# Row maxima of a 16384 x 1024 matrix: coarser loads, seven rows by way of TensorE and GpSimd, a split last row and a later first store

## The chip, the cores and the metric

The kernel runs on one core of one Trainium2 chip. The metric is the device time of one execution in microseconds; a smaller one is better. Times "from the start" are counted from the beginning of the profiled span.

## The reference

```python
def setup_inputs():
    batch, seq, dim = 32, 512, 1024
    return {
        "x": np.random.randn(batch, seq, dim).astype(np.float32),
    }

def reference(x: np.ndarray) -> np.ndarray:
    return np.max(x, axis=-1).astype(np.float32)
```

The input is 32 x 512 x 1024 float32, 67.1 MB; the output is the maximum of each of the 16384 rows of 1024 elements.

## The kernel before, in words

The 16384 rows are spread over 128 partitions, 128 rows to each. They are cut in two blocks (`BLOCKS`, L13). In the first, partition p holds 112 consecutive rows of the input, in the second 16. Within a block the rows of a partition are brought in by loads of n consecutive rows each: one DMA (L49) brings n x 1024 elements to each of the 128 partitions, n x 4 KB in one piece. The list has 15 loads of 14 down to 3 rows, and then 11 of 2 and 1 rows.

The loads go into `ring` (L37), one tile with room for 46 rows in each partition. `at` is the next free row; where a load doesn't fit before the end, it begins at row 0 again (L46, L47). A load that lands on rows used earlier must wait until the reductions of those rows are done. The scheduler puts that wait on SP, which issues all loads in the order of the list; it also gives each DMA one of eight completion semaphores in turn, and a DMA that gets a semaphore again waits for the one that had it before.

For each load VectorE runs one `reduce_max` over the free dimension (L50): n maxima per partition from n x 1024 elements, written into `res` (L38), 128 columns of one value each. VectorE works on the loads in their order and waits for each load's semaphore. No other engine computes. ScalarE issues the two stores (L54), each behind its block's last reduction: 112 values of each partition, and 16.

So three queues set the order: SP's list of loads, VectorE's list of reductions, and ScalarE's two stores. TensorE and GpSimd have nothing but the start and the end of the program.

Of the kernel before, what the change touches and what calls it, by code (L numbers as in the profile page):

```python
# [1 line left out]

# [4 lines left out]


F32 = mybir.dt.float32

BLOCKS = [  # L13
    [14, 14, 12, 11, 9, 8, 8, 7, 6, 5, 4, 4, 4, 3, 3],
    [2, 2, 2, 2, 2, 1, 1, 1, 1, 1, 1],
]
RING = 46


@with_exitstack  # L20
def kernel(
    ctx: ExitStack,
    tc: tile.TileContext,
    x: bass.AP,
    out: bass.AP,
):
    nc = tc.nc
    P = 128
    X = mybir.AxisListType.X

    xf = x.flatten_outer_dims()
    N, D = xf.shape
    I = N // P
    of = out.flatten_outer_dims()

    once = ctx.enter_context(tc.tile_pool(name="once", bufs=1))
    ring = once.tile([P, RING, D], F32)  # L37
    res = once.tile([P, I], F32)  # L38

    at = first = 0  # L40
    for loads in BLOCKS:
        S = sum(loads)
        xb = xf[first * P:(first + S) * P, :].rearrange("(p i) d -> p i d", p=P)
        b = 0
        for g in loads:
            if at + g > RING:  # L46
                at = 0  # L47
            xc = ring[:, at:at + g, :]
            nc.sync.dma_start(out=xc, in_=xb[:, b:b + g, :])  # L49
            nc.vector.reduce_max(out=res[:, first + b:first + b + g], in_=xc, axis=X)  # L50
            at += g
            b += g
        dst = bass.AP(tensor=of.tensor, offset=of.offset + first * P, ap=[[S, P], [1, S]])
        nc.scalar.dma_start(out=dst, in_=res[:, first:first + S])  # L54
        first += S
    assert first == I


# [1 line left out]
_INS = ['x']  # L60
_OUTS = [((32, 512), 'float32')]


# [23 lines left out]
```

## Time and profile before

| | |
|---|---|
| median of 9 runs | 165.04 us (165.00 to 165.17) |
| the profiled execution, its own time | 165.17 us |
| its span in the profile | 163.4 us |
| VectorE busy | 138.5 us, 26 reductions |
| DMA, loads' queue | 67.11 MB, 96.4% of 16 engines' span |
| first reduction begins | 20.24 us |
| last reduction ends | 160.96 us |
| last store issued | 161.00 us |

How to read it: the profiled span lies within the execution; 1.77 us of its time are outside. A busy share of DMA is the mean over the core's 16 DMA engines. The profile calls VectorE DVE, TensorE PE, ScalarE ACT and GpSimd POOL; "SPq" and "ACTq" are the instruction queues that issue DMAs, which aren't counted as busy. In the groups of instructions `res<-ring` means that `res` is written and `ring` read, and the idle time behind the last bar is what the engine waited just before the group's instructions.

### The profile page before, as it was taken

How to read it: one execution, taken by the hardware profiler on the slowest of the kernel's cores; microseconds unless marked ns; L12 is line 12 of the kernel's file. 1: busy time of each engine (PE TensorE's matmuls, PEld its weight loads, DVE VectorE, ACT ScalarE, POOL GpSimd, SP SyncE). 2: the span in 40 equal slices, each digit the busy share in tenths (PEclk: the TensorE clock that was granted, in tenths of full speed). 3: DMA queues.
4: the chain of work that ended last, by engine and by line, in shares of the span. 5: the costliest groups of instructions: out<-in, count | busy, mean ns of one | idle time of the engine just before them, and what ended most of it. 6: DMA issues, size and time to landing. Idle time of an engine off the chain costs nothing.

```text
span 163.4 us, 109 instructions
## 1 busy us (share of the span) xinstructions
DVE 138.5 (85%) x26; POOL 0.2 (0%) x4
## 2 busy tenths in 40 slices
DVE  0000099968999999999999999999999999999994
POOL 0000000000000000000000000000000000000000
DMA  6999999998899897999989999999999999999980
GB/s 225 449 449 449 449 449 449 449 417 385 385 421 509 353 529 321 433 433 473 441 385 481 417 442 428 413 400 451 416 429 421 437 418 420 421 420 415 407 348 2
DMA packets 4032, 67.18 MB, mean 411 GB/s; under 512 B 704, under 2 KB 704, under 8 KB 1472
## 3 DMA queue, kind: packets, MB, share of 16 engines
q1 hardware_dynamic: 3744, 67.11, 96.4%
q10 hardware_dynamic: 288, 0.07, 0.2%
HBM read 67.11 MB, written 0.07 MB: 411 GB/s over the span
## 4 chain that ended last, share of the span: by engine, by line
DMA 57%; DVE 40%; DVEq 1%; SPq 0%; issue 0%
DMA ring<-in_x_dram 57%; DVE res L50 40%; DVEq L82 1%; SPq L49 0%
## 5 line engine op out<-in xcount | busy, mean ns | idle before, releaser
L50 DVE TENSOR_REDUCE res<-ring 128x1 f32<-128x1024 f32 (+11 forms) x26 | 138.5, 5398 | 22.5 <-DMA ring<-in_x_dram 22.5
L71 POOL MEMSET const-bfloat16-1.0<- 128x1 bf16 x1 | 0.1, 102 | 0.0
L71 POOL MEMSET const-uint8-127<- 128x1 uint8 x1 | 0.1, 101 | 0.0
L71 POOL MEMSET const-float32-0.0<- 128x1 f32 x1 | 0.1, 99 | 0.2 <-issue 0.2
L71 POOL MEMSET const-float32-1.0<- 128x1 f32 x1 | 0.1, 98 | 0.0
## 6 DMA issues: line engine op xcount, KB each, us to landing
ring<-in_x_dram SPq DMA_DIRECT2D x2, 7168.0 KB, 27.7
ring<-in_x_dram SPq DMA_DIRECT2D x2, 4096.0 KB, 31.6
ring<-in_x_dram SPq DMA_DIRECT2D x1, 6144.0 KB, 50.1
ring<-in_x_dram SPq DMA_DIRECT2D x3, 2048.0 KB, 36.8
ring<-in_x_dram SPq DMA_DIRECT2D x1, 5632.0 KB, 29.7
ring<-in_x_dram SPq DMA_DIRECT2D x5, 1024.0 KB, 24.6
ring<-in_x_dram SPq DMA_DIRECT2D x1, 4608.0 KB, 23.6
ring<-in_x_dram SPq DMA_DIRECT2D x1, 3584.0 KB, 38.3
```

Source lines behind the costliest of these rows:

```text
L50: nc.vector.reduce_max(out=res[:, first + b:first + b + g], in_=xc, axis=X)
L71: nc = _bacc.Bacc("TRN2", target_bir_lowering=False, num_devices=1)
L82: with _tile.TileContext(nc) as tc:
```

## The change

The lists of loads change: 22 whole loads (15, 15, 15, 15, 14, 11, 11, 8, 4, 4 rows, then three of 2 and nine of 1) instead of 26, and the very last row of each partition comes in two loads of half a row. The ring has 45 rows instead of 46.

The last row: the first half goes to the ring and its maximum is written to the element just ahead of the second half in a tile `tail`; the last reduction then covers that element and the second half, 513 elements.

Seven rows of each partition no longer go through VectorE's long reductions: the last two rows of load seven (11 rows), the last three of load eight (8 rows) and the last two of load ten (4 rows). For each such row `turn` has TensorE transpose eight 128 x 128 pieces into PSUM, ScalarE copy the 128 x 1024 result to SBUF, and GpSimd take the maximum over the partitions with an all-reduce. After it element c x 128 + p of every partition is the maximum of piece c of partition p's row. `back` has TensorE turn the eight 1 x 128 pieces of partition 0 into columns of a small PSUM tile, and a short VectorE reduction over eight values per row (the merge) writes the maxima into `res`. The merges stand on VectorE's queue after loads nine, thirteen and seventeen. TensorE's and VectorE's orders are fixed by hand (`in_turn`). An identity matrix for the transposes is made on VectorE ahead of the first reduction, in eight instructions. The program of GpSimd gains a library reload ahead of seven all-reduces, that of ScalarE a table load and seven copies.

The first block's store is issued behind the reduction of the last whole row, and the second block's store follows it, both still on ScalarE's queue.

```diff
 BLOCKS = [
-    [14, 14, 12, 11, 9, 8, 8, 7, 6, 5, 4, 4, 4, 3, 3],
-    [2, 2, 2, 2, 2, 1, 1, 1, 1, 1, 1],
+    [15, 15, 15, 15, 14, 11, 11, 8, 4, 4],
+    [2, 2, 2, 1, 1, 1, 1, 1, 1, 1, 1, 1],
 ]
-RING = 46
+RING = 45
+TENSOR = {
+    6: [("turn", 6, 0), ("turn", 6, 1), ("back", 6, 0), ("back", 6, 1)],
+    7: [("turn", 7, 0), ("turn", 7, 1), ("turn", 7, 2), ("back", 7, 0), ("back", 7, 1)],
+    9: [("turn", 9, 0), ("turn", 9, 1), ("back", 7, 2), ("back", 9, 0), ("back", 9, 1)],
+}
+BY_GPSIMD = {6: 2, 7: 3, 9: 2}
+MERGE = {8: 6, 12: 7, 16: 9}
...
+    def turn(j, k):
+        rows, cols = tiles[j]
+        ps = psum.tile([P, D], F32)
+        for c in range(C):
+            in_turn("PE", nc.tensor.transpose(
+                out=ps[:, c * P:(c + 1) * P],
+                in_=rows[:, k, c * P:(c + 1) * P],
+                identity=ident,
+            ))
+        sb = turned.tile([P, D], F32)
+        nc.scalar.copy(out=sb, in_=ps)
+        top = allr.tile([P, D], F32)
+        nc.gpsimd.partition_all_reduce(top, sb, P, bass_isa.ReduceOp.max)
+        tops[j, k] = top
+
+    def back(j, k):
+        if j not in backs:
+            fetched = psmall.tile([P, BY_GPSIMD[j], C], F32)
+            backs[j] = fetched
+        for c in range(C):
+            in_turn("PE", nc.tensor.transpose(
+                out=backs[j][:, k, c:c + 1],
+                in_=tops[j, k][0:1, c * P:(c + 1) * P],
+                identity=ident[0:1, 0:1],
+            ))
...
-            nc.vector.reduce_max(out=res[:, first + b:first + b + g], in_=xc, axis=X)
+            cols = res[:, first + b:first + b + n]
+            m = BY_GPSIMD.get(j, 0)
+            tiles[j] = xc[:, n - m:, :], cols[:, n - m:]
+            for what, i, k in TENSOR.get(j, []):
+                (turn if what == "turn" else back)(i, k)
+            reduce = in_turn("DVE", nc.vector.reduce_max(
+                out=cols[:, :n - m], in_=xc[:, :n - m, :], axis=X))
+            if j in MERGE:
+                i = MERGE[j]
+                in_turn("DVE", nc.vector.reduce_max(out=tiles[i][1], in_=backs[i], axis=X))
...
-        nc.scalar.dma_start(out=dst, in_=res[:, first:first + S])
...
+    half = ring[:, at, :H]
+    nc.sync.dma_start(out=half, in_=xb[:, b, :H])
+    nc.sync.dma_start(out=tail[:, PAD:], in_=xb[:, b, H:])
+    in_turn("DVE", nc.vector.reduce_max(out=tail[:, PAD - 1:PAD], in_=half, axis=X))
+    in_turn("DVE", nc.vector.reduce_max(out=res[:, I - 1:], in_=tail[:, PAD - 1:], axis=X))
+
+    store = nc.scalar.dma_start(out=views[0][0], in_=views[0][1])
+    tc.add_manual_dep(store.ins, reduce.ins.name, SYNC, reason="behind the loads")
+    nc.scalar.dma_start(out=views[1][0], in_=views[1][1])
```

The code counts loads from 0, so its load 6 is load seven here, 7 is eight and 9 is ten.

## Prediction

> **What bounds the kernel now.** I read the page's engine row and queue rows first, then stretches of the span, the chain that ended last, the groups by shape (line, operation, shapes, count | busy us, mean ns | idle before) and the DMA queue's waits.
>
> ```profile
> DVE 138.5 (85%) x26; POOL 0.2 (0%) x4
> ...
> q1 hardware_dynamic: 3744, 67.11, 96.4%
> q10 hardware_dynamic: 288, 0.07, 0.2%
> ```
>
> The loads fill 96.4% of what sixteen DMA engines have in the span. VectorE is busy for less, but starts late, as the stretches (us from the start: length, VectorE busy, GpSimd busy, clock, DMA share, GB/s) show:
>
> ```profile
> 0.00:20.24 20.24, 0.00 (x1) 0.20 (x4) 1.00 0.98 408
> 20.24:37.19 16.95, 15.09 (x2) 0.00 (x0) 1.00 0.98 425
> 37.19:95.20 58.01, 57.99 (x5) 0.00 (x0) 1.00 0.99 428
> 95.20:142.90 47.70, 47.52 (x10) 0.00 (x0) 1.00 1.00 426
> ```
>
> After 20.24 us of waiting for the first 14 rows VectorE is nearly never idle, and neither is DMA: two bounds lie on each other. The chain's last pieces (start, length) say which is late at the end:
>
> ```profile
> 131.98 19.92 DMA ring<-in_x_dram
> 151.90 0.02 issue
> 151.92 7.92 DVE res L50 x6
> 159.84 1.13 DVEq L82
> ```
>
> The last load that VectorE waits for is ready at 151.90. Six one-row loads follow; in the trace's single DMA packets they take 7.67 us together, so the last is ready at about 159.57. VectorE ends seven reductions 9.04 us after 151.92, at 160.96, and began the last at 159.75: 0.18 us behind DMA.
>
> ```profile
> L50 DVE TENSOR_REDUCE res<-ring 128x14 f32<-128x14336 f32 x2 | 30.2, 15086 | 22.1 <-DMA ring<-in_x_dram 22.1
> ...
> L50 DVE TENSOR_REDUCE res<-ring 128x2 f32<-128x2048 f32 x5 | 11.1, 2282 | 0.2 <-DMA ring<-in_x_dram 0.2
> ...
> L50 DVE TENSOR_REDUCE res<-ring 128x1 f32<-128x1024 f32 x6 | 6.8, 1209 | 0.0
> ```
>
> SP's own waits (total us, times, longest):
>
> ```profile
> SPq L49 <- DVE res L50: 77.6, 7, 15.1
> ...
> SPq L49 <- DMA out_dram<-res: 5.0, 1, 5.0
> ```
>
> A lone reduction of n rows takes 0.143 + 1.067n us (1.209 and 15.086); back to back, starts lie 1.067n + 0.06 apart (the timeline has 15.00 us between a 14-row and the next). SP waits 77.6 us for ring slots and 5.0 us for the store, yet DMA stays at 0.98 to 1.00, since loads are queued far ahead. In the packets a load of 14, 8, 4, 2, 1 rows takes 16.91, 9.71, 4.89, 2.48, 1.28 us: 1.202n + 0.08.
>
> [...]
>
> **The change, part by part**, against the profiled execution (span 163.4, its time 165.17, so 1.77 outside; the median 165.04 is 0.13 lower).
>
> *Loads.* 26 become 24, with the same bytes: 2 x 0.08 = 0.16 us less DMA. They are queued by SP alone, as before. Ready times: the first 15 rows at 20.24 + 1.20 = 21.44; then 39.6, 57.7, 75.8 (15 rows each), 92.7 (14), 106.0 and 119.3 (11), 129.0 (8), 133.9 and 138.8 (4), 141.3, 143.8, 146.2 (2). Ring of 45: load four waits for the first reduction's end, 37.5, while two loads are queued to 57.7; load six for 73.8 (queued to 92.7); load seven for 91.9 (to 106.0); load eight for 107.7 (to 119.3). So DMA doesn't run dry: 0, on the cover of at least 11 us of queued loads.
>
> *Store of block one.* Its 128 packets of 448 B take 25 ns each, 8 per engine: 0.20 us out of the load stream. The 5.0 us wait of SP hid behind queued loads: 0. It goes out at the end of the last whole row's reduction, about 159.0; ACT issues for 0.34 us, so it is free before the last store's turn at 160.2. Cost 0; at most 0.3 if the last store queues behind it.
>
> *Last row in halves.* The last reduction is 513 elements: 0.143 + 0.53 = 0.68 instead of 1.21 us. The first half's reduction (0.6 us) runs while the second half lands, 0.68 us; a DMA-bound end thus comes at 159.57 - 0.16 - 0.20 + 0.68 = 159.89, 1.07 earlier than 160.96.
>
> *VectorE.* Larger first loads alone would make it late: 1.2 us later start, and after the first four loads it waits 2.0 us each time, for a 15-row load takes 18.1 us to land and 16.1 to reduce. It ends load five at 107.7, 1.7 after load six is ready. Seven rows less are 7.47 us: it ends load six at 119.5, seven (9 rows) 129.2, eight (5) 134.6, nine (4) 138.9, a merge, ten (2 rows) at 141.3, just when the next load is ready. The 2-row loads set the pace to 146.2 + 2.2 = 148.4. Then a merge, four rows, a merge and five rows: 9 x 1.127 + 0.3 = 10.4, at 158.8; the halves 0.6 + 0.7: 160.2 us (0.1 from rounding). So VectorE ends last, 0.75 us earlier than before. A merge reads 16 or 24 PSUM elements: below the one-row 0.143 us floor is unlikely, I take 0.15, from 0.06 to 0.3: -0.25 to +0.4 in all. The eight set-up instructions lie in the 21 us before the first load: 0 (cover gone, about 1 us).
>
> *The side path.* Row by row: eight transposes[...], a ScalarE copy of 1024 elements out of PSUM (estimate: 1.0, near VectorE's 1.07 for 1024), an all-reduce on GpSimd, and eight one-column transposes back[...]. [...] With 3.1 us: load seven's two rows start at 119.3, are at GpSimd at 122.7, end at 128.9, and are back at 130.1; VectorE asks at 138.9. PE holds load eight's turns behind the wait for those (its queue is in order), so they begin at 130.1, GpSimd ends four and five at 139.7 and 142.8; the turns of load ten go ahead of the fifth's way back, which is done at 146.2 (asked at 148.4), and the last pair is back at 151.5 (asked at 153.1). No stall, the smallest margin 1.6 us. If the wait bites, what is queued behind it on VectorE is every later row and the last store.
>
> *Library and instruction fetch.* [...] I take 0.1[...].
>
> Sum: -0.75 + 0.1 = -0.65: 165.17 - 0.65 = 164.5 on the profiled scale, 164.4 on the median's.
>
> **The rivals.**
> 1. *Forecast, 66%*: the side path is in time, VectorE or DMA ends at 159.9 to 160.5: 163.9 to 164.7. For it: the margins above; against: no row prices GpSimd.
> 2. *Gain eaten, 13%*: the path is in time, but the reload, fetches or dearer merges take back 0.5 to 1 us. For it: DMA has no gap in which to hide bytes, VectorE none after 148. About 165.0, between 164.7 and 165.4.
> 3. *GpSimd becomes the bound, 21%*: the merges for loads eight and ten stall VectorE. With the turns at 2.2 us it decides from an all-reduce of 3.35 us on. Above that, each further microsecond costs six (six all-reduces and no slack): at 4 us VectorE ends near 164.2, the kernel at 168.4; at 5 us near 170.7 and 175. Turns of 4.4 us would do the same (170.4, so 174.6). For it: the margin is 1.6 us in 32[...].
> That the change doesn't do what it says is hardly open: the order of instructions has seven all-reduces and three merges.
>
> **How the numbers follow.** About 0.2% is what a measurement here can tell from no change, 0.33 us. Faster is case 1, 0.66; same is case 2, 0.13; slower is case 3, 0.21[...]. About 4% lies under 163.8, and of case 3 only its edge under 166.0 belongs in the range: 163.8 to 166.0.
>
> **What would show it.** Right: VectorE busy near 132, no wait for PE at the merges, last reduction under 0.7 us ending at 160.2, both stores after 159, DMA share still 0.98 or more up to 158. All-reduces started less than 3.4 us apart confirm the side path. Wrong: VectorE waits for PE before a merge; [...]DMA gaps after 37 us (the ring); the last store over 1.5 us from issue to landing.

## The result, and the profile after

The changed kernel takes 165.85 us (median of 9 runs, 165.76 to 166.07) against 165.07 us of the kernel before, measured beside it (29 runs). The ratio is 1.0048, 95% interval 1.0040 to 1.0057: 0.78 us slower, where 0.65 us less had been forecast. The profiled execution took 165.91 us, its span 164.1.

The page's engine row and queue rows of the changed kernel come first.

```profile
PE 17.4 (11%) x112; PEld 16.2 (10%) x112; DVE 134.0 (82%) x35; ACT 8.4 (5%) x8; POOL 22.7 (14%) x11
...
q1 hardware_dynamic: 3456, 67.11, 95.8%
q10 hardware_dynamic: 288, 0.07, 0.2%
q8 instruction: 1, 0.02, 0.0%
```

VectorE is busy for 4.5 us less than the 138.5 before, where about 6.5 less had been forecast ("near 132"): the eight set-up instructions, 1.6 us of busy time on this page, had been left out of that figure. They end 2.5 us from the start, and after them VectorE still waits 18.8 us for the first load, so they cost no time. The last row has no partner before: one packet (one piece that a DMA engine moves) on a queue named "instruction". Next, the side path in the groups by shape.

```profile
L106 POOL PARTITION_ALL_REDUCE top<-sb x7 | 22.5, 3267 | 127.2 <-ACT sb L104 127.2
...
L104 ACT COPY sb<-ps 128x1024 f32<-128x1024 f32 x7 | 7.1, 1012 | 136.0 <-PE ps L98 134.3 <-POOL top L106 1.7
...
L143 DVE TENSOR_REDUCE res<-fetched 128x2 f32<-128x16 f32 x2 | 0.3, 166 | 0.0
L143 DVE TENSOR_REDUCE res<-fetched 128x3 f32<-128x24 f32 x1 | 0.2, 174 | 0.0
```

The last column of the merges (L143) is 0.0: VectorE waited for none of them. Its waits (total us, times, longest) say the same: all of them are for loads, apart from 0.8 us at the start.

```profile
DVE res L139 <- DMA ring<-in_x_dram: 26.2, 8, 18.8
DVE ident L76 <- PEq L176: 0.8, 1, 0.8
```

So the part of the prediction that had no row to stand on, the side path, came in on time, and the loss is elsewhere. The chain of the changed kernel ends so (start, length):

```profile
148.90 10.22 DMA ring<-in_x_dram
159.12 0.02 issue
159.14 1.22 DVE res L139
160.37 0.60 DVE tail L155
160.97 0.02 issue
160.99 0.69 DVE res L156
```

VectorE waits until 159.12 for the last whole row, and the end is 161.68 instead of the 160.2 of the forecast. By the prediction's sums that load should have been ready near 157.85 (159.21 less two half rows of 0.68). It is DMA that is 1.3 us late, though it moves the same bytes. The stretches of the changed kernel at the end show how (length; busy times of PE, of PEld, which is TensorE's loading of weights, DVE, ACT and POOL; clock; DMA share; GB/s):

```profile
157.60:158.40 0.80, 0.00 (x0) 0.00 (x0) 0.75 (x2) 0.00 (x0) 0.00 (x0) 0.50 0.88 323
158.60:159.00 0.40, 0.00 (x0) 0.00 (x0) 0.40 (x1) 0.00 (x0) 0.00 (x0) 0.50 0.07 26
159.00:159.40 0.40, 0.00 (x0) 0.00 (x0) 0.35 (x2) 0.00 (x0) 0.00 (x0) 0.50 0.07 26
```

A share of 0.07 is one engine of sixteen, which here moves 26 GB/s: fifteen are done by 158.60, and one works on alone. In the trace's packets of the last loads it ends at 159.96, 1.37 us after the others. The delay fits the instruction packet, which this answer on the DMA queues of the changed kernel, cut to 146.3 to 146.8 us, contains:

```profile
q1 hardware_dynamic: 57, 0.20, 101.4%
q8 instruction: 1, 0.02, 13.7%
```

The packet has 16384 bytes and took 1.10 us, from 146.56 to 147.66. The row's packet that begins just as it ends, at 147.64, took 0.44 instead of 0.16 us, and one at 148.07 took 0.36. With the 0.28 and 0.20 us that these two took longer, the packet's 1.10 makes 1.58; the one engine is late by 1.37, about a row's packet less, as if one had run beside the instruction packet, which isn't shown. Each load ends with sixteen packets of 4 bytes (384 for the 24 loads). For the last whole row the late engine's comes at 158.67, the other fifteen's by 157.25, and VectorE's wait ends after the late one, at 159.12. So this load was ready only when its slowest engine was done. From load fourteen, the first to end after the packet, to the last half row the late engine's 4 bytes come 1.37 to 1.42 us after the other fifteen: every later load is late by as much.

### The profile page after: what moved, and what is told of

It is laid out like the page before. It is cut to its first block, busy times and chain, and to the rows that moved or that the text cites. A ratio compares the mean times of both kernels' runs of the same rounds, so it can differ in the third digit from the quotient of the medians.

```text
span 164.1 us, 368 instructions
## 1 busy us (share of the span) xinstructions
PE 17.4 (11%) x112; PEld 16.2 (10%) x112; DVE 134.0 (82%) x35; ACT 8.4 (5%) x8; POOL 22.7 (14%) x11
## 4 chain that ended last, share of the span: by engine, by line
DMA 69%; DVE 28%; SPq 1%; issue 0%
DMA ring<-in_x_dram 69%; DVE res L139 27%; SPq L133 1%; DVE res L156 0%; DVE tail L155 0%
## 5 line engine op out<-in xcount | busy, mean ns | idle before, releaser
L139 DVE TENSOR_REDUCE res<-ring 128x1 f32<-128x1024 f32 (+7 forms) x22 | 131.0, 5969 | 26.7 <-DMA ring<-in_x_dram 26.2
L106 POOL PARTITION_ALL_REDUCE top<-sb x7 | 22.5, 3267 | 127.2 <-ACT sb L104 127.2
L98 PE MATMUL ps<-ident,ring 128*128 128x128 f32 x56 | 11.7, 397 | 119.4 <-DMA ring<-in_x_dram 119.4
L98 PEld LDWEIGHTS ps<-ident,ring 128*128 128x128 f32 x56 | 10.8, 216 | 119.4 <-issue 119.4
L104 ACT COPY sb<-ps 128x1024 f32<-128x1024 f32 x7 | 7.1, 1012 | 136.0 <-PE ps L98 134.3
L115 PE MATMUL fetched<-ident,top 1*128 1x1 f32 x56 | 6.0, 223 | 14.3 <-POOL top L106 14.3
L115 PEld LDWEIGHTS fetched<-ident,top 1*128 1x128 f32 x56 | 5.4, 179 | 15.5 <-POOL top L106 15.3
L156 DVE TENSOR_REDUCE res<-tail 128x1 f32<-128x513 f32 x1 | 0.7, 686 | 0.0
L155 DVE TENSOR_REDUCE tail<-ring 128x1 f32<-128x512 f32 x1 | 0.7, 676 | 0.0
L143 DVE TENSOR_REDUCE res<-fetched 128x2 f32<-128x16 f32 (+1 forms) x3 | 0.5, 169 | 0.0
```

The costliest lines, as they stand in the source:

```text
L98: in_turn("PE", nc.tensor.transpose(out=ps[:, c * P:(c + 1) * P], in_=rows[:, k, c * P:(c + 1) * P], identity=ident,))
L104: nc.scalar.copy(out=sb, in_=ps)
L106: nc.gpsimd.partition_all_reduce(top, sb, P, bass_isa.ReduceOp.max)
L115: in_turn("PE", nc.tensor.transpose(out=backs[j][:, k, c:c + 1], in_=tops[j, k][0:1, c * P:(c + 1) * P], identity=ident[0:1, 0:1],))
L139: reduce = in_turn("DVE", nc.vector.reduce_max(out=cols[:, :n - m], in_=xc[:, :n - m, :], axis=X))
L143: in_turn("DVE", nc.vector.reduce_max(out=tiles[i][1], in_=backs[i], axis=X))
```

## The experiments

**Theory**: the packet of 16384 bytes carries a part of TensorE's longer program through one of the DMA engines that bring the loads; as DMA's share in the changed kernel is 1.00, 0.99 and 1.00 from 40 to 75, to 110 and to 152 us, that engine has no gap in which to catch up. **Rival 1**: the half-row loads leave one engine behind. **Rival 2**: the traffic of TensorE, ScalarE and GpSimd on SBUF slows an engine.

**One transpose back instead of eight.** This kernel leaves out seven of the eight transposes back of each of the seven rows, and so takes their maxima over an eighth of their elements. The edit:

```diff
-        for c in range(C):
+        for c in range(1):
             in_turn("PE", nc.tensor.transpose(
                 out=backs[j][:, k, c:c + 1],
...
-                in_turn("DVE", nc.vector.reduce_max(out=tiles[i][1], in_=backs[i], axis=X))
+                in_turn("DVE", nc.vector.reduce_max(out=tiles[i][1], in_=backs[i][:, :, 0:1], axis=X))
```

> The changed kernel with one transpose back per offloaded row instead of eight; seven eighths of those rows' maxima are left out. TensorE's program falls from 112 to 63 transposes, everything else stays. Theory (one 16 KB instruction fetch of TensorE's program on one DMA engine holds that engine, and with it every later load, back by 1.3 us): no packet on the instruction queue, all sixteen engines end together, VectorE ends near 160.3 instead of 161.7, time 164.5. Rival 1 (the half-row loads themselves make one engine late): one engine still ends 1.3 us after the others, 165.8. Rival 2 (TensorE, ScalarE and GpSimd reading SBUF slow a DMA engine): likewise 165.8, since the same bytes go through all three.

Measured: 164.52 us, ratio to before 0.9968 (0.9955 to 0.9980). The queue rows of this kernel's page have no instruction packet:

```profile
q1 hardware_dynamic: 3456, 67.11, 96.5%
q10 hardware_dynamic: 288, 0.07, 0.2%
```

and its chain ends 1.2 us earlier:

```profile
147.69 10.23 DMA ring<-in_x_dram
157.92 0.02 issue
157.94 1.22 DVE res L139
159.16 0.60 DVE tail L155
159.76 0.02 issue
159.79 0.69 DVE res L156
```

Between 158.6 and 159.0 us DMA's share is 0.03, not 0.07:

```profile
158.60:159.00 0.40, 0.00 (x0) 0.00 (x0) 0.40 (x1) 0.00 (x0) 0.00 (x0) 0.50 0.03 10
```

The half rows, all turns, copies and all-reduces are still there, so both rivals fall. Without the packet the change would have gained about 0.55 us (165.07 - 164.52); the packet takes 165.85 - 164.52 = 1.33 us. The transposes that are left out can't be the price themselves, as VectorE waited for no merge in the changed kernel.

**The program's length alone, on the kernel before.** An identity is made as in the change, and then, with PE_N = 112:

```diff
...
+    for n in range(PE_N):
+        c = n % (D // P)
+        nc.tensor.transpose(out=ps[:, c * P:(c + 1) * P], in_=ident, identity=ident)
```

> The kernel before, with an identity made on VectorE at the start and 112 transposes of it on TensorE, which nothing waits for: TensorE's program is as long as the changed kernel's, and no load, store or reduction is changed. Theory: one instruction packet of 16 KB within the first 40 us, one engine late by 1.1 to 1.3 us from there on, and VectorE, only 0.2 us behind DMA before, ends about 1.2 us later: 166.2. Rivals 1 and 2 (half-row loads, reads of the ring by other engines): unchanged, 165.0 to 165.1.

Measured: 166.60 us, ratio 1.0092 (1.0078 to 1.0105), 1.53 us more. The queue rows on this kernel's page:

```profile
q1 hardware_dynamic: 3744, 67.11, 95.7%
q10 hardware_dynamic: 288, 0.07, 0.2%
q8 instruction: 1, 0.02, 0.0%
```

The packet runs from 17.4 to 18.4 us (0.94 us), and the loads' packet that begins as it ends took 2.61 instead of 2.12 us (DMA's share from 18 to 20 us is 1.08, against 1.06 from 15 to 17). No load, reduction or store is other than before, nothing waits for TensorE, and TensorE is finished by 18 us; yet 140 us later the chain has not made it good:

```profile
153.08 0.02 issue
153.10 7.92 DVE res L72 x6
161.02 1.13 DVEq L104
```

The corresponding pieces before began at 151.92 and 159.84, so these are 1.2 us later. It is so all the way: the second reduction begins at 38.37 against 37.19. The fetch costs about as much at 17 us (1.53) as at 147 (1.33), and it needs no rows of the input on TensorE. The profiled executions differ by 1.40 us (166.57 against 165.17), the medians by 1.53; what lies between these and the 1.2 of the chain isn't explained.

**A shorter and a longer program.** PE_N = 80, 96 and 224 in the same kernel:

> The kernel before with 80 idle transposes on TensorE instead of 112 (160 instructions with the weight loads, instead of 224). Theory (the length of the program decides, through the fetch): no instruction packet, all sixteen DMA engines together, 165.0 to 165.2. Rival (idle TensorE work as such, its clock or its start, costs the 1.5 us): about 1.5 x 80/112 = 1.1 us more than before, 166.2.

> The kernel before with 96 idle transposes, 192 instructions. The changed kernel's packet came when TensorE had done about 96 transposes of 112, the one with 112 idle transposes after about 105. Theory: no packet or a packet too late to matter, 165.1; with a packet 166.6. Either bounds the length at which the fetch sets in, between 80 and 96 or between 96 and 112.

> The kernel before with 224 idle transposes, 448 instructions. Theory: two instruction packets of 16 KB or more. If they go to one DMA engine the delays add up, 2 x 1.5 over before: 168.1; if to two engines, each is late by itself and the loads wait for the later one: 166.6, as with 112.

| transposes | instructions with weight loads | instruction packets in the profile | time, us | ratio to before (95%) |
|---|---|---|---|---|
| 80 | 160 | 0 | 165.23 | 1.0009 (1.0003 to 1.0016) |
| 96 | 192 | 0 | 165.31 | 1.0028 (1.0005 to 1.0050) |
| 112 | 224 | 1 | 166.60 | 1.0092 (1.0078 to 1.0105) |
| 224 | 448 | 1 | 166.85 | 1.0106 (1.0090 to 1.0122) |

It is a step and not a slope: 80 to 112 transposes cost 1.4 us, 112 to 224 another 0.25. The work of 80 transposes as such, with the set-up, costs 0.1 us, and not the 1.1 of the rival in that expectation. With 96 four of five runs lie at 165.22 to 165.41, one at 166.42: on the edge, as if the packet came in that run alone; there is no trace of that run, so this is an inference. For 224 the expectation was wrong: not two packets, but one.

That the packet carries instructions of TensorE is inferred from its queue's name on the page and from this step; no trace shows its content, nor why it comes at a length near 96 to 112 transposes. The table counts matmuls and weight loads alone, and the profile leaves register, branch and semaphore instructions out of its counts. The packet costs 1.33 us in the changed kernel and 1.53 in the kernel before with 112 transposes.

**The parts by themselves.** The changed kernel without its side path:

```diff
-TENSOR = {
...
-BY_GPSIMD = {6: 2, 7: 3, 9: 2}
-MERGE = {8: 6, 12: 7, 16: 9}
+TENSOR = {}
+BY_GPSIMD = {}
+MERGE = {}
```

> The changed kernel's loads, half rows and store order, with the seven rows reduced by VectorE and no side path at all. By the prediction's sums VectorE then has 7.47 us more rows and 0.45 us less merges, ends near 167.2, time 171.3 to 171.6. Theory: no instruction packet, and the sixteen engines end together though the half rows are there. Rival 1: one engine 1.3 us after the others, as in the changed kernel.

Measured: 170.72 us, ratio 1.0341 (1.0322 to 1.0359), 0.6 less than the lower figure expected: VectorE ends at 166.6, 0.6 earlier than summed. The half-row loads are in it, and between 158.6 and 159.0 us DMA's share is 0.00: they leave no engine behind. What the coarse loads cost VectorE, the side path gives back: without it 4.9 us more than the changed kernel.

And the split last row and the later first store alone, with the lists of loads and the ring of before (the edit against the kernel before):

```diff
-    [2, 2, 2, 2, 2, 1, 1, 1, 1, 1, 1],
+    [2, 2, 2, 2, 2, 1, 1, 1, 1, 1],
...
+    half = ring[:, at, :H]
+    nc.sync.dma_start(out=half, in_=xb[:, b, :H])
+    nc.sync.dma_start(out=tail[:, PAD:], in_=xb[:, b, H:])
...
+    tc.add_manual_dep(store.ins, reduce.ins.name, SYNC, reason="behind the loads")
```

> The list of loads of the kernel before with the last row in halves and the first store behind the loads, without the side path: the first of the two edits alone. VectorE is 0.18 us behind DMA at the end before; the halves cost it one more start (0.06), the store's packets leave DMA (0.2). Theory: VectorE bounds the end, 164.9, a gain of 0.1 to 0.2 us. If the end were set by DMA: 164.1.

Measured: 165.20 us, ratio 1.0010 (1.0002 to 1.0018): 0.1 us slower, where 0.1 to 0.2 us less was expected. Its chain ends:

```profile
126.97 24.68 DMA ring<-in_x_dram
151.65 0.02 issue
151.67 7.75 DVE res L119 x6
159.42 0.09 issue
159.51 0.69 DVE tail L135
160.19 0.02 issue
160.22 0.69 DVE res L136
```

The later store did give DMA its time: VectorE's last wait ends at 151.65, 0.25 us before the 151.90 of the kernel before. From there VectorE works without a pause to 160.91, 9.24 us where the kernel before takes 9.04 (151.92 to 160.96): the extra start of the second half eats the lead. With VectorE as the bound, splitting the last row gains nothing here; where the 0.1 us more is lost isn't settled.

**A version without the fetch.** Five rows by the side path, 80 transposes, and loads to match (the edit against the changed kernel):

```diff
-    [15, 15, 15, 15, 14, 11, 11, 8, 4, 4],
-    [2, 2, 2, 1, 1, 1, 1, 1, 1, 1, 1, 1],
+    [15, 15, 14, 14, 13, 11, 9, 9, 5, 5, 2],
+    [2, 2, 1, 2, 1, 1, 1, 1, 1, 1, 1, 1],
...
-BY_GPSIMD = {6: 2, 7: 3, 9: 2}
-MERGE = {8: 6, 12: 7, 16: 9}
+BY_GPSIMD = {7: 2, 9: 3}
+MERGE = {9: 7, 15: 9}
```

> The whole change with five rows instead of seven by way of TensorE and GpSimd (80 transposes), and the loads 15, 15, 14, 14, 13, 11, 9, 9, 5, 5, 2 rows, then 2, 2, 1, 2 and eight of 1, so that VectorE keeps pace with two more rows. 25 loads and two halves... one load more than the changed kernel, 0.08 us. Theory: no instruction packet, merges without a stall, VectorE ends near 160.5, 164.6: faster than both kernels. If the side path costs something other than its fetch: 165.5 or more.

Measured: 164.85 us (21 runs), ratio to before 0.9984 (0.9977 to 0.9990), without an instruction packet. It is the fastest of the kernels that do the whole work: 1.0 us less than the changed kernel and 0.26 us less than the one before. (The expectation miscounts its loads: they are 23 whole ones and two halves, 25 in all, against 24 of the changed kernel.) Its VectorE ends at 160.50, as forecast for it, with no pause after 147.71:

```profile
147.71 3.41 DVE res L138 x2
151.12 0.09 DVE res L142
151.21 7.97 DVE res L138 x7
159.18 0.60 DVE tail L154
159.78 0.02 issue
159.81 0.69 DVE res L155
```

The time is 0.25 us above the 164.6 expected. As the lists of loads differ too, the 1.0 us is not the price of the fetch by itself.

## Why the prediction was wrong, point by point

- **The step that failed** is "Library and instruction fetch". Its 0.1 us was the author's estimate, with no row of a trace behind it, for GpSimd's library ahead of the first reduction; an instruction packet in the middle of the run, at 146.56 us, is priced nowhere. The runs put 1.33 us in the place of 0.1 (165.85 against 164.52 without the packet): the packet held an engine for 1.10 us and the two behind it took 0.28 and 0.20 longer. The library costs nothing that shows: VectorE began with the first 15 rows at 21.27 us, forecast 21.44, and with the second 15 at 39.39, against 39.43 in the kernel without side path and library.
- With that term set to 1.33, the forecast's own sum is -0.75 + 1.33 = +0.58; measured is +0.78. The missing 0.2 us has the size of the error in the next point.
- **The tail** was set 0.2 to 0.3 us too early. VectorE was summed from 148.4 as 9 x 1.127 + 0.3, as if it never waited again; but one-row loads come every 1.28 us, so it waits for the last whole row until 157.92 even without the fetch. Then 1.22, 0.60 and 0.69 follow: 160.48, not 160.2. The DMA-bound 159.89 was out of reach too, since the last whole row's 1.22 us don't fit under the 0.68 us of the first half.
- **The side path** was right, though the forecast's 3.1 us for an all-reduce and 2.2 us for a row's turn were the author's assumptions, shown by no trace of the kernel before. All-reduces began 3.21 us apart (6.43 us for two in the timeline), the copy took 1.01 (forecast 1.0), the first 16 transposes 3.64 us, 1.82 per row, eight back 0.66 to 1.01, a merge 0.17 (forecast 0.15). The first pair's way back ended at 129.96 (130.1), the last at 151.13 (151.5), asked for at 153.89. No merge waited. That 3.21 lies so near the assumed 3.1 is luck. The rival's 175 us at an all-reduce of 5 us is 0.6 more than six for each further microsecond gives from its 168.4; nothing came to depend on it.
- **VectorE's own sums** were right to 0.2 us up to the merge after load nine: 92.63, 107.63 and 138.80 against 92.7, 107.7 and 138.9. (The wait after load four is 0.8 and not 2.0 us, as the forecast's own ready time of 92.7 has it.) The ring didn't hold DMA, as forecast: its share is 0.99 from 37 to 152 us, though SP waited longer for slots than before, 89.6 us against 77.6.
- **The rivals.** "Gain eaten" was the one that came, by one of the three causes it named, fetches; it stopped at 165.4 because it let them take back no more than 1 us. GpSimd as the bound, which had the larger chance, did not come. The range to 166.0 held the median; the direction and the size were wrong.

## What to carry to other kernels

Here, with DMA's share at 0.98 to 1.00 in the stream of loads, one packet of 16384 bytes of TensorE's own program lengthened the run by 1.33 and 1.53 us. Where DMA is the bound, count the instructions that an edit adds, here to TensorE, and look on the page for an "instruction" queue. One delayed engine of sixteen delayed each load that waited for all sixteen, and with no pause in the stream the delay stayed to the end, here for 140 us (1.2 us late at 38 us and 1.2 at 161). Where the loads' pace and VectorE's lie on each other, as here with one-row loads every 1.28 us and one-row reductions of 1.22, sum the tail from the last load that is really waited for, not from the engine's work alone.

## What the runs showed of the hardware that had not been expected

- An instruction packet of 16384 bytes took 1.10 us in the changed kernel and 0.94 us in the kernel before with 112 idle transposes, on one DMA engine beside full loads, and the loads' packets behind it took longer too (0.44 and 0.36 instead of 0.16 us; one of 2.61 instead of 2.12). It cost these kernels 1.33 and 1.53 us. With 224 and with 448 instructions of TensorE one such packet came; with 160 none came, and with 192 none in the profile, though one run of five was 1.1 us longer than the others.
- A GpSimd all-reduce of 128 x 1024 float32 took 3.21 us beside a busy VectorE, and slowed it by nothing that shows: a 9-row reduction took 9.75 us, with all-reduces running for 6.43 us of it, and 9.74 us before.
- 80 idle transposes on TensorE, without a fetch, cost 0.1 us in 165 (ratio 1.0009).
